# A decoder layer's front: from a planner's order to one written by hand, 76 half tiles of weights with attention staged between them

## The chip, the cores and the metric

The kernel runs on one core of a Trainium2 chip. TensorE does the matrix products, VectorE and ScalarE the elementwise work, GpSimd some elementwise work and some transfers; SyncE issues the transfers of the weights. Each engine takes its instructions from a queue of its own, in order. The metric is the device time of one execution in microseconds (us).

## The reference

One layer of a decoder with 256 tokens, width 2048 and float32 weights. Two kinds of attention read the same normed input, eight latent heads (MLA) and sixteen window heads (SWA) with sinks and a relative bias; then comes an MLP of width 8192.

```python
a = rms_norm(h, attn_norm)
c_q, c_kv, k_rope, q_s, k_s, v_s = split(a @ w_in)
# latent heads: causal softmax over all keys
q  = rms_norm(c_q, q_a_norm) @ w_q_b       # 8 x (128 plain + 64 rotated)
kv = rms_norm(c_kv, kv_a_norm) @ w_kv_b    # 8 x (128 keys + 128 values)
s  = (q_nope . k_nope + rope(q_rope) . rope(k_rope)) * 192 ** -0.5
y_mla = softmax(causal(s)) @ v
# window heads: 16 queries, 2 keys and values, 128 tokens back, a sink per head
s = q_s . k_s * 64 ** -0.5 + rel_bias[t5_bucket(pos_q - pos_k)]
m = max(max(s), sink);  e = exp(s - m)
y_swa = e / (sum(e) + exp(sink - m)) @ v_s
h = h + concat(y_mla, y_swa) @ w_out
h = h + square(relu(rms_norm(h, mlp_norm) @ w_up)) @ w_down
out = rms_norm(h, final_norm)
```

## The kernel before

Every activation and every weight is split into a high and a low part, so that three products of reduced precision make one of full precision. A weight part of 128 x 1024 values is loaded by SyncE into `raw`, copied to its high part `hi` on ScalarE (line 104) and subtracted to its low part `lo` on VectorE (line 105). `raw`, `hi` and `lo` have four buffers each. One chunk of a product is a pair of matmuls, 512 and 256 columns (lines 114 and 116). `load_block` loads two parts, `mm_tile` multiplies a whole tile.

The front goes in this order. `in0` (lines 252 to 271): keys, values and the first two query tiles of the window heads, in 16 chunks as the input arrives. 15 tiles of `w_in` (lines 519 to 558): six query tiles, four tiles of `c_kv`, four of `c_q`, one of the rotated key. Two blocks each of `w_kn` (latent keys) and `w_v` (latent values), three of `w_q_b`; then `w_out` in two halves of 16 tiles, the first over the window heads' output, the second over the latent heads'. The MLP follows: 64 tiles of `w_up` and 64 of `w_down`, two weight parts each.

Attention lies between these tiles. `buckets` makes the bucket of each token distance in 16 compare steps, `lanes_load` spreads them, `bias_step` makes a one-hot row from them and multiplies it with the bias table, and `bias_load` brings the result back through DRAM. `x_norm` makes the norm of the input and scales keys, values and queries by it. For each of eight window head pairs `swa_scores` does the split, the scores and the softmax (lines 380 to 429), and `swa_pv` the transposes and the product with the values (lines 431 to 450). For a latent head `mla_split`, `mla_scores` and `mla_pv` do the same (lines 600 to 663). `c_norm` norms the latent tiles, `rope` rotates. GpSimd subtracts the low parts of queries and keys (lines 387, 604 and 613), rotates (lines 508 and 509) and adds squares (line 187).

The calls are written in the order above, but the order in each engine's queue is the planner's: the framework takes from the written program what it expects to be ready, the earliest written first.

## Time and profile before

| | us |
|---|---|
| three runs | 1030.43, 1031.1, 1032.51 |
| their median | 1031.1 |
| the profiled execution | 1032.6 |
| its span, first to last instruction | 1030.8 |
| TensorE busy in it | 1008.3 |
| VectorE busy | 705.0 |
| ScalarE busy | 539.5 |
| GpSimd busy | 105.7 |

The profile is one execution. Its views used here are the page's busy times, a table of busy time per stretch, the list of waits of an engine, groups of equal instructions, and the timeline. A matmul's end is modelled, and matmuls overlap at their ends, so a duration is longer than the step from one matmul to the next. The first matmul of the `w_in` tiles starts at 30.4 us, the first of `w_out` at 202.1, the first of `w_up` at 308.1.

### The profile page before, as it was taken

To read this page: it belongs to the slowest core of one execution; us is meant where nothing else is said; L and a number is where in the kernel's file an instruction comes from. 1 tells how busy PE (TensorE), PEld (TensorE's weight loads), DVE (VectorE), ACT (ScalarE), POOL (GpSimd) and SP (SyncE) were. 2 spreads that over 40 slices of the span, in tenths; PEclk is the share of its full clock that TensorE was granted. 3 is DMA by queue.
4 is the path that set the end of the run, shared out by engine and by line. 5 is a ranking of instruction groups with operands and counts; after the bars stand their busy time and mean duration, and the time that the engine had idled before them with its cause. 6 is when DMAs were issued, how large, how long until landed. Compare 5 with 4: busy or idle time off the path is not lost.

```text
span 1030.8 us, 15494 instructions
## 1 busy us (share of the span) xinstructions
PE 1008.3 (98%) x5854; PEld 886.8 (86%) x5854; DVE 705.0 (68%) x1123; ACT 539.5 (52%) x893; POOL 105.7 (10%) x112
## 2 busy tenths in 40 slices
PE   9989789999999999999999999999999999999997
PEld 8878678889888888888888888888888888888887
DVE  7895589798897866655566656566666556666664
ACT  6675599965664444333444433344443334445553
POOL 2121340551232200000000000000000000000000
PEclk9999899999999999999999999999999999999999
DMA  8957523353454655555555555555555555555552
GB/s 299 317 206 210 155 91 141 135 188 129 161 185 164 216 192 185 193 193 187 187 195 191 185 192 195 184 189 198 186 185 195 192 185 191 196 185 187 194 172 82
DMA packets 53450, 191.04 MB, mean 185 GB/s; under 512 B 6096, under 2 KB 6480, under 8 KB 52864
## 3 DMA queue, kind: packets, MB, share of 16 engines
q1 hardware_dynamic: 51840, 184.57, 51.1%
q0 software_dynamic: 1392, 5.41, 2.2%
q8 instruction: 46, 0.75, 0.3%
q14 instruction: 28, 0.23, 0.1%
q10 hardware_dynamic: 144, 0.07, 0.0%
HBM read 185.80 MB, written 4.23 MB: 184 GB/s over the span
## 4 chain that ended last, share of the span: by engine, by line
PE 85%; DMA 4%; DVE 4%; ACT 4%; issue 2%; POOL 0%; ACTq 0%; POOLq 0%; DVEq 0%
PE up L114 23%; PE dn L114 22%; PE up L116 12%; PE dn L116 11%; PE wo L114 5%; PE wo L116 3%; DMA raw_in<-in_w_in_dram 2%; DMA bias<-bias_scratch 2%; PE in L114 2%; DVE lo_in L105 1%; PE in L116 1%; PE dn L764 1%; PE yp L444 1%; ACT st L422 0%; DVE buck L243 0%
## 5 line engine op out<-in xcount | busy, mean ns | idle before, releaser
L114 PE MATMUL up<-ms,hi_up 128*128 128x512 f32 x1024 | 355.4, 392 | 0.0
L116 PE MATMUL up<-ms,lo_up 128*128 128x256 f32 x1024 | 287.7, 281 | 0.0
L104 ACT CAST hi_dn<-raw_dn 128x1024 fp32r<-128x1024 f32 x128 | 134.3, 1049 | 201.6 <-PE dn L114 161.2
L105 DVE TENSOR_TENSOR lo_up<-raw_up,hi_up 128x1024 fp32r<-128x1024 f32 x128 | 161.1, 1259 | 114.0 <-ACT hi_up L104 113.6
L114 PEld LDWEIGHTS up<-ms,hi_up 128*128 128x128 f32 x1024 | 192.1, 188 | 42.1
L104 ACT CAST hi_up<-raw_up 128x1024 fp32r<-128x1024 f32 x128 | 134.2, 1049 | 174.3 <-issue 133.6
L105 DVE TENSOR_TENSOR lo_dn<-raw_dn,hi_dn 128x1024 fp32r<-128x1024 f32 x128 | 156.9, 1226 | 96.1 <-ACT hi_dn L104 91.0
L116 PEld LDWEIGHTS up<-ms,lo_up 128*128 128x128 f32 x1024 | 192.5, 188 | 0.0
L114 PE MATMUL dn<-usB,hi_dn 128*128 128x512 f32 x496 | 174.9, 392 | 0.0
L114 PE MATMUL dn<-usC,hi_dn 128*128 128x512 f32 x496 | 174.9, 392 | 0.0
L116 PE MATMUL dn<-usB,lo_dn 128*128 128x256 f32 x496 | 139.4, 281 | 0.0
L116 PE MATMUL dn<-usC,lo_dn 128*128 128x256 f32 x496 | 139.4, 281 | 0.0
L114 PEld LDWEIGHTS dn<-usB,hi_dn 128*128 128x128 f32 x496 | 93.1, 188 | 20.4
L114 PEld LDWEIGHTS dn<-usC,hi_dn 128*128 128x128 f32 x496 | 93.1, 188 | 20.4
L116 PEld LDWEIGHTS dn<-usB,lo_dn 128*128 128x128 f32 x496 | 93.2, 188 | 0.0
L116 PEld LDWEIGHTS dn<-usC,lo_dn 128*128 128x128 f32 x496 | 93.2, 188 | 0.0
L114 PE MATMUL wo<-ys,hi_wo 128*128 128x512 f32 x256 | 90.5, 395 | 0.2 <-DVE mla L323 0.2
L114 PE MATMUL in<-xs,hi_in 128*128 128x512 f32 x240 | 86.9, 400 | 0.0
L116 PE MATMUL wo<-ys,lo_wo 128*128 128x256 f32 x256 | 72.4, 284 | 0.0
L116 PE MATMUL in<-xs,lo_in 128*128 128x256 f32 x240 | 68.8, 287 | 0.7 <-DVE lo_in L105 0.7
L105 DVE TENSOR_TENSOR lo_in<-raw_in,hi_in 128x1024 fp32r<-128x1024 f32 (+1 forms) x39 | 47.7, 1224 | 17.4 <-ACT hi_in L104 17.2
L114 PEld LDWEIGHTS wo<-ys,hi_wo 128*128 128x128 f32 x256 | 48.0, 188 | 10.4 <-DVE mla L323 0.5
(298 smaller groups left out, 1261.3 us busy)
## 6 DMA issues: line engine op xcount, KB each, us to landing
raw_up<-in_w_up_dram SPq DMA_DIRECT2D x128, 512.0 KB, 3.6
raw_dn<-in_w_down_dram SPq DMA_DIRECT2D x128, 512.0 KB, 3.6
raw_in<-in_w_in_dram SPq DMA_DIRECT2D x37, 512.0 KB, 6.0
raw_wo<-in_w_out_dram SPq DMA_DIRECT2D x32, 512.0 KB, 4.2
raw_qb<-in_w_q_b_dram SPq DMA_DIRECT2D x6, 512.0 KB, 3.7
xt<-in_x_tok_dram SPq DMA_DIRECT2D x2, 1024.0 KB, 8.1
bias_scratch<-biasT POOLq DMA_DIRECT2D x4, 512.0 KB, 5.3
bias<-bias_scratch POOLq DMA_DIRECT2D x4, 512.0 KB, 9.9
```

What stands on the lines that cost most here:

```text
L104: nc.scalar.copy(hi[:, :n], raw[:, :n])
L105: nc.vector.tensor_tensor(lo[:, :n], raw[:, :n], hi.bitcast(F32)[:, :n], op=ALU.subtract)
L114: nc.tensor.matmul(ps[:, 0:2 * S], lhsT=hi[:, col:col + P], rhs=act(k, 0, 2 * S), start=first, stop=False)
L116: nc.tensor.matmul(ps[:, S:2 * S], lhsT=lo[:, col:col + P], rhs=act(k, 0, S), start=False, stop=last)
L444: nc.tensor.matmul(yp[:, 0:S], lhsT=v_sc[:, 0, t // 4, j, :], rhs=pt[:, j, 0:2, :].rearrange("p i c -> p (i c)"), start=(j == 0), stop=False)
L764: nc.tensor.matmul(ps[:, b * S:(b + 1) * S].rearrange("p (a c) -> p a c", a=2), lhsT=hi[:, (k % 8) * P:(k % 8 + 1) * P], rhs=x[:, :, b, :] ...
```

## The change

Everything after `in0` and before the MLP is written as one region in which each engine's instructions run in the order in which they are written. The unit is a half: one weight part of 128 x 1024, 76 of them (30 of `w_in`, 4 of `w_kn`, 4 of `w_v`, 6 of `w_q_b`, 32 of `w_out`). A half's matmuls are eight pairs (twelve products of 512 columns for `w_v`). Tables say which step stands ahead of a half's weights (`pre`), which goes into its matmuls at which pair (`hook`), and which follows (`post`).

Besides: the bucket steps are gone, the one-hot row is made from the distance itself by `abs(distance - middle) < half width` of each bucket; the bias goes out and back in pieces of 16 rows; the input's norm loads in four pieces of 1024 columns through the `raw` buffers. The norms are folded: the window scores are scaled per query while the bias is added, values while they are copied from their transposes, and the latent tiles aren't scaled at all, with the `EPS` under their own root scaled instead. The softmax's last scaling goes from ScalarE to one VectorE operation. The product with the values writes two heads into the two partition halves with 64 weight columns each; the first block's and the previous block's share go through one product, with the own block's values replaced by a difference. All subtractions, rotations and adds of GpSimd go to VectorE. The squares for the MLP's norm and the scaling of `h` move into the first 16 `w_up` tiles.

```diff
-    def buckets(step):
...
+    def distances():
...
+        nc.vector.tensor_scalar(dist, n_f[:, 0:2, :], 0.0, 255.0, op0=ALU.max, op1=ALU.min)
+        nc.gpsimd.dma_start(scratch.rearrange("i q c -> q i c"), dist)
...
+    def oh_away(n):
...
+        nc.scalar.activation(oh, lanes[o // 4096][:, o % 4096:o % 4096 + 512], AF.Abs,
+                             bias=c_sb[:, 4:5])
+    def oh_hot(n):
+        nc.vector.tensor_scalar(oh, oh.bitcast(F32), c_sb[:, 5:6], None, op0=ALU.is_lt)
...
+    def swa_max(t):
...
+        for w, other in ((1, bias[:, 0, hs, :]), (0, st[:, :, 0, :])):
+            nc.vector.scalar_tensor_tensor(st[:, :, 0, :], av[:, :, w, :], rx8[:, 0:1], other,
+                                           op0=ALU.mult, op1=ALU.add)
...
+    def swa_norm(t):
...
+        nc.vector.tensor_tensor(st4, st4, l.unsqueeze(2).broadcast_to([P, 4, P]), op=ALU.mult)
...
+    def swa_pv(t):
...
+            nc.tensor.matmul(yp[j * 64:(j + 1) * 64, 0:S], lhsT=vv[:, 0, kv],
+                             rhs=pt[:, j, :, :].rearrange("p i c -> p (i c)"),
+                             start=True, stop=False)
...
+    def mla_lo(hd):
...
+            nc.vector.tensor_tensor(qk[:, i, 0, :], mla[:, row, :], qk.bitcast(F32)[:, i, 1, :],
                                     op=ALU.subtract)
...
+    for i in range(15):
+        e = 2 * i + 2
+        if i < 6:
+            at(pre, e, q_out, 2 + i)
+        elif i < 14:
+            which, c = ("kv", i - 6) if i < 10 else ("q", i - 10)
+            at(pre, e, c_out, which, c, i)
+            at(post, e + 1, c_square, which, c)
...
+            at(pre, e, wo_out, half, mt)
...
+    for n in range(16):
+        s_ = 2 + n // 2
+        at(post, s_, oh_away, n)
+        at(pre, s_ + 1, oh_hot, n)
+        pe(s_ + 1, 3 + 3 * (n % 2), bias_mm, n)
+        at(pre, s_ + 2, bias_out, n)
+    at(post, 13, bias_mask)
...
+    at(post, 16, k_lo)
+    for t in range(8):
+        b = 17 + 3 * t
+        at(pre, b - 1, lambda t=t: stack_hi(f"qs{t}", q_sb[t]))
+        at(post, b - 1, lambda t=t: stack_lo(f"qs{t}", q_sb[t]))
+        pe(b, 1, swa_mm, t)
+        at(post, b, swa_max, t)
+        at(pre, b + 1, swa_exp, t)
+        at(post, b + 1, swa_norm, t)
+        pe(b + 2, 1, swa_turn, t)
+        at(post, b + 2, swa_pt, t)
+        pe(b + 3, 1, swa_pv, t)
+        at(post, b + 3, y_out, NH_MLA + t)
+    for which, s_, g0, sc, dst in (("kv", 22, G_KV, 1.0, ckv_at),
+                                   ("q", 30, G_Q, (128 + 64) ** -0.5, cq_at)):
+        pe(s_, 3, c_sums, which)
+        at(post, s_, c_mean, which)
+        at(pre, s_ + 1, rsqrt_a, which)
+        at(post, s_ + 1, c_scales, which, sc)
+        pe(s_ + 2, 3, bcast, which)
+        for i in range(LC):
+            at(post, s_ + 2 + i // 2, c_apply, which, i, g0)
+            at(pre, s_ + 3 + i // 2, c_hi, which, i, dst)
+            at(post, s_ + 3 + i // 2, c_lo, which, i, dst)
...
+    for hd in range(8):
+        a = 41 + 2 * hd
+        at(post, a, mla_hi, hd)
+        at(pre, a + 1, mla_lo, hd)
+        pe(a + 1, 3, mla_mm, hd)
+        at(post, a + 1, mla_max, hd)
+        at(pre, a + 2, mla_exp, hd)
+        at(post, a + 2, mla_norm, hd)
+        pe(a + 3, 1, mla_turn, hd)
+        at(post, a + 3, mla_pt, hd)
+        pe(a + 4, 1, mla_pv, hd)
+        at(post, a + 4, y_out, hd)
...
+    with tc.manual_schedule():
+        for n in range(3):
+            w_hi(n)
+        for n in range(2):
+            w_lo(n)
+        for s_ in range(NS + 2):
+            for f in pre.get(s_, ()):
+                f()
+            if s_ + 3 < NS:
+                w_hi(s_ + 3)
+            if s_ + 2 < NS:
+                w_lo(s_ + 2)
+            if s_ < NS:
+                mms[s_](s_, weights.pop(s_))
+            for f in post.get(s_, ()):
+                f()
```

`w_hi(n)` issues the load of half `n` and its copy on ScalarE, `w_lo(n)` its subtraction on VectorE. `pe(s, k, f)` puts `f` ahead of pair `k` of half `s`. `stack_hi` and `stack_lo` split a query tile; `mla_hi` and `mla_lo` a latent head's query and key, and for even heads the rotated query as well.

## Rows read from the trace of the kernel before

**Rows 1.** The page's part 1: busy us, share of the span, instructions.

```profile
PE 1008.3 (98%) x5854; PEld 886.8 (86%) x5854; DVE 705.0 (68%) x1123; ACT 539.5 (52%) x893; POOL 105.7 (10%) x112
```

**Rows 2.** Busy time by stretch: us, busy per engine, clock, DMA share, GB/s.

```profile
30.40:100.00 69.60, 66.36 (x375) 56.63 (x374) 53.49 (x101) 46.77 (x75) 15.07 (x21) 1.00 0.75 237
100.00:130.00 30.00, 23.27 (x127) 20.12 (x127) 15.15 (x38) 16.21 (x47) 10.64 (x10) 0.89 0.62 160
130.00:202.00 72.00, 67.70 (x390) 58.25 (x388) 61.39 (x148) 69.07 (x187) 22.93 (x24) 1.00 0.33 117
202.00:308.10 106.10, 105.41 (x633) 93.42 (x634) 95.92 (x178) 67.09 (x133) 36.97 (x34) 1.00 0.48 168
...
400.00:700.00 300.00, 300.00 (x1732) 264.35 (x1732) 184.14 (x240) 126.06 (x152) 0.00 (x0) 1.00 0.54 190
```

**Rows 3.** Waits of TensorE: us in total, times, the longest.

```profile
PE tp L435 <- ACT st L428: 4.4, 1, 4.4
...
PE sb L396 <- DVE st L404: 2.4, 1, 2.4
```

**Rows 4.** Timeline of TensorE, 127 to 136: start, us, instruction.

```profile
127.18 1.02 PE L444 MATMUL yp<-pt,v_sc 128*128 128x256 f32 x4
...
128.49 0.50 PE L195 MATMUL ts_kv<-ones,acc_kv 128*128 128x1 f32 x4
128.85 0.48 PE L392 MATMUL sa<-kk,qs 128*128 128x256 f32 x2
...
129.64 0.28 PE L116 MATMUL in<-xs,lo_in 128*128 128x256 f32 x1
129.76 0.40 PE L114 MATMUL in<-xs,hi_in 128*128 128x512 f32 x1
...
134.73 0.60 PE L435 MATMUL tp<-ident,st 128*128 128x128 f32 x4
135.08 0.48 PE L114 MATMUL in<-xs,hi_in 128*128 128x512 f32 x1
```

**Rows 5.** Timeline of TensorE at 218, a latent head's scores and the transposes after.

```profile
218.00 0.28 PE L625 MATMUL ms<-qk 128*128 128x256 f32 x1
...
218.94 0.49 PE L652 MATMUL mtp<-ident,mst 128*128 128x128 f32 x3
```

**Rows 6.** Timeline of TensorE at 55, bias matmul (64 weight columns) and next pair.

```profile
55.05 0.39 PE L302 MATMUL bias<-oh,rel_hi 128*64 128x512 f32 x1
...
55.51 0.39 PE L114 MATMUL in<-xs,hi_in 128*128 128x512 f32 x1
```

**Rows 7.** Timeline of VectorE at 425, in the MLP; the second needs the first.

```profile
425.78 0.42 DVE L683 TENSOR_TENSOR h<-dn,h 128x256 f32<-128x256 f32 x1 [0.59 <-PE dn L116]
426.24 0.42 DVE L684 TENSOR_TENSOR h<-dn,h 128x256 f32<-128x256 f32 x1
426.75 1.23 DVE L105 TENSOR_TENSOR lo_dn<-raw_dn,hi_dn 128x1024 fp32r<-128x1024 f32 x1
```

**Rows 8.** Timeline of VectorE at 139, steps that don't wait for one another.

```profile
139.41 0.41 DVE L403 TENSOR_TENSOR st<-sa,bias 128x256 f32<-128x256 f32 x1
...
141.06 0.68 DVE L409 TENSOR_REDUCE nm<-st 128x4 f32<-128x512 f32 x1
```

**Rows 9.** Groups of ScalarE, 0 to 330: busy us, mean ns, idle before.

```profile
L104 ACT CAST hi_wo<-raw_wo 128x1024 fp32r<-128x1024 f32 x32 | 33.3, 1048 | 14.6 <-PE wo L114 12.9 <-ACT ms L137 0.6 <-ACT hi_wo L104 0.6
```

**Rows 10.** Timeline of ScalarE at 133, the first exponential and what follows the fourth.

```profile
133.69 0.40 ACT L422 ACTIVATE st<-st,nm 128x128 f32<-128x128 f32 x1
...
135.44 0.80 ACT L142 CAST ckvn<-cn_kv 128x256 fp32r<-128x256 f32 x2
```

**Rows 11.** Groups of GpSimd: busy us, mean ns, idle before.

```profile
L604 POOL TENSOR_TENSOR qk<-mla,qk 128x256 fp32r<-128x256 f32 x16 | 16.9, 1076 | 30.6 <-ACT qk L603 23.4 <-issue 7.1
```

**Rows 12.** The page's part 6, transfers: times, KB each, us to landing.

```profile
bias_scratch<-biasT POOLq DMA_DIRECT2D x4, 512.0 KB, 5.3
bias<-bias_scratch POOLq DMA_DIRECT2D x4, 512.0 KB, 9.9
```

More of the change, by code (lines that the diff above doesn't have):

```diff
@@ new lines, in diag, with bcast @@
+    def diag(name):
+        for b in range(2):
+            dg = work.tile([P, P], F32, tag="diag", name=f"dg_{name}_{b}", bufs=2)
+            nc.vector.tensor_scalar(dg, ident, box[f"y_{name}"][:, b:b + 1], None, op0=ALU.mult)
+            box[f"dg_{name}_{b}"] = dg
+    def bcast(name):
+        ps = misc_ps(f"bc_{name}")
+        for b in range(2):
+            nc.tensor.matmul(ps[:, b * P:(b + 1) * P], lhsT=ones, rhs=box[f"dg_{name}_{b}"],
+                             start=True, stop=True)
+        box[f"bc_{name}"] = ps
@@ new lines, in wo_mm, with mm, in0_out, q_out @@
+    def wo_mm(half, mt):
+        def mm(s_, w):
+            ps = dense_ps(f"wo{half}_{mt}")
+            act = view(ys[1 - half])
+            for k in range(8):
+                run_hooks(s_, k)
+                pair(ps, w, k * P, act, k, k == 0, k == 7)
+            opened[f"wo{half}_{mt}"] = ps
+        return mm
+    def in0_out(j):
+        t = evac_sum(ps0[j], f"in0_{j}")
+        nc.vector.tensor_tensor(first[j], ps0[j][:, 0:S], t, op=ALU.add)
+    def q_out(t):
+        q_sb[t] = work.tile([P, S], F32, tag="q_s", name=f"q_s{t}", bufs=8)
+        sum_evac(q_sb[t], opened.pop(t - 2), f"q{t}")
@@ new lines, in v_out, with wo_out, ms_hi @@
+    def v_out(b):
+        for tb in range(2):
+            nc.scalar.copy(box["mla"][:, VV + 4 * tb + 2 * b:VV + 4 * tb + 2 * b + 2, :],
+                           opened[f"v{b}"][tb].rearrange("p (a c) -> p a c", a=2))
+    ms_box = []
+    def wo_out(half, mt):
+        residual(opened.pop(f"wo{half}_{mt}"), mt)
+    def ms_hi(mt):
+        if not ms_box:
+            ms_box.append(big.tile([P, KC, 2 * S], F32R, tag="A", name="ms"))
+        nc.scalar.activation(ms_box[0][:, mt, 0:S], h[:, mt, :], AF.Copy,
+                             scale=g_sb[:, G_MLP + mt:G_MLP + mt + 1])
@@ new lines @@
+    W0 = len(srcs)
+    for half in range(2):
+        for mt in range(KC):
+            e = plan(w_out[half, mt // 2][:, (mt % 2) * WH:(mt % 2 + 1) * WH], wo_mm(half, mt)) + 1
+            at(pre, e, wo_out, half, mt)
+            if half == 1:
+                at(post, e, ms_hi, mt)
+                at(pre, e + 1, ms_lo, mt)
+    NS = len(srcs)
+    for j, s_ in ((2, 0), (3, 0), (0, 1), (1, 1)):
+        at(pre, s_, in0_out, j)
+    at(pre, 2, rope_a)
+    at(pre, 3, rope_b, 0)
+    at(pre, 4, rope_b, 1)
@@ new lines @@
+    at(pre, 5, rope_c)
+    at(post, 5, rope_d)
+    for n in range(16):
[5 more added lines that the diff above has]
+    at(post, 13, bias_mask)
+    for n in range(4):
+        at(pre, 9 + n, x_piece, n % 2, n // 2)
+    at(pre, 13, x_mean)
+    at(pre, 13, rsqrt_a, "x")
+    at(pre, 14, x_scales)
+    pe(14, 2, v_turn)
+    pe(14, 6, bcast, "x")
+    at(pre, 15, x_apply)
@@ new lines @@
+    at(pre, 15, v_scale)
+    at(post, 15, k_hi)
+    at(post, 15, v_diff)
+    at(post, 16, k_lo)
[11 more added lines that the diff above has]
+        at(post, b + 3, y_out, NH_MLA + t)
```

633 lines of the change are left out of this document (351 added, 282 removed).

## The prediction

> **What bounds the kernel now.** I read the page's busy shares first. TensorE is busy 98% of the span [rows 1], so no change can give more than TensorE's idle and slow time, unless it takes matmuls away. The windows by stage, cut where the work changes (input groups to 30.4 us, `w_in` tiles to about 149, `w_kn`, `w_v` and `w_q_b` to 202, `w_out` to 308.1, then the MLP), show where that time lies [rows 2]: 3.2, 6.7, 4.3 and 0.7 us idle in the four windows between 30.4 and 308.1, 15.0 in all, and from 400 us on none. In 100:130 the granted clock is 0.89 on the mean, so for some of it the lower level, 1.2 GHz, after a wait of 4.4 us; 11% of 30 us is another 3.3 us. The waits of TensorE name the causes [rows 3]: transposes waiting for a softmax, scores waiting for VectorE.
>
> How much could go? I price the matmuls alone. A pair (512 and 256 columns) takes 300 us / 866 pairs = 0.3464 us where nothing is idle [rows 2]. A head pair of the window attention takes 1.31 us for `swa_pv`'s products (127.18 to 128.49), 0.79 for the scores (128.85 to 129.64), 0.35 for four transposes (134.73 to 135.08) [rows 4]: 2.45. A latent head takes 0.94 for its scores (218.00 to 218.94) [rows 5], three quarters of 0.35 for its transposes and half of 1.31 for its products: 1.85. A 512-column matmul alone takes half of 0.46 [rows 6]. From 30.4 us: 576 pairs 199.5, 48 of `w_v` 10.9, 32 for the bias 7.3, 8 head pairs 19.6, 8 heads 14.8, some 2.3 for the norms; together 254.4. They would end at 284.8 and they end at 308.1: **23.3 us** is lost, of which the windows show 18.3 and the rest is the drain before each wait. That is all the change can win, as it takes no matmul away.
>
> **What the change does to each engine.** TensorE keeps all its matmuls. The spots at which it asks for attention operands are now fixed: one pair into a half, or three. The MLP and the tail stay, except that 15 adds and the scaling of `h` go from GpSimd to VectorE in the first 16 `up` tiles; VectorE is busy 184 of 300 us in such a stretch [rows 2], so I cost them at nothing; without that cover they are some 11 us of VectorE.
>
> VectorE loses the 16 bucket steps, the scaling by the input norm of 6 tiles and 11 projections, and the masking of the previous block. It gains 56 two-input operations that GpSimd does now (40 low parts of queries and keys, 10 steps of rotations, 6 folds of squares), and the softmax's last scaling, from ScalarE. GpSimd's take 1.08 us each [rows 11], VectorE's 0.42 and a weight subtraction 1.23 [rows 7].
>
> **How the queues go.** In written order each half is the same: evacuations and conversions (`pre`), the weight copy for three halves on (ScalarE) and subtraction for two halves on (VectorE), the half's matmuls, then `post`. `pre` waits for the last matmul of the half before. So an engine starts each half when TensorE does, and what stands last in `post` must be done when TensorE reaches the next half's first hook. My rules: a 256-wide VectorE operation lasts 0.42 and the next, if independent, issues 0.33 later (139.41 to 141.06 for five) [rows 8]; a dependent one comes 0.46 later [rows 7], a hand-over of 0.04, which I round to 0.05; a reduction lasts 0.68 [rows 8]; ScalarE copies a half in 1.05 [rows 9]; four exponentials take 1.75 (133.69 to 135.44) [rows 10]; a matmul's result comes 0.16 after its issue slot (0.28 - 0.12) [rows 4]. A half of eight pairs is 2.77 us.
>
> **Halves 2 to 10** (bias). The one-hot compare stands behind the rotation's angle steps (four 256-wide operations, three dependent ones, three and a clamp). In half 3 they take 1.4 us ahead of it and half 2 has run over, so the bias matmul waits 1.5; in half 4 with an evacuation ahead as well, 2.2; then 0.5 in three halves that have an evacuation. Sum **5.1**. The key norm and first stacks, halves 14 to 17: four key subtractions and two stack ones, 2 us, follow the weight in half 16: **1.6**.
>
> **Window attention** (halves 17 to 41, three to a head pair). From the end of its scores: result at 0.21; mask and bias steps 0.48 + 0.35 + 0.48 + 0.48, reduction 0.73, two small ones 0.42, so 3.15; sink 0.1 and four exponentials to 4.98; sum, reciprocal, the 512-wide scaling (0.69) to 6.24. TensorE meanwhile issues 7 + 8 + 1 = 16 pairs, 5.54 us, then asks for the scaled scores: at least 0.70 lost, eight times, **5.6**. Twice (halves 21 and 27) the square of a latent tile stands on ScalarE behind exponentials and weight copy, and its add on VectorE ahead of the scaling: 1.5 each, **3.0**. And VectorE is too full. Its issue time for a head pair is three weights at 1.14, 3.4, and 5.4 for the steps above, the stack, the masked own block and the output's low part, against TensorE's 3 x 2.77 + 2.45 = 10.8. Where the latent norms, the rotated key and the `w_kn` evacuations fall, 4.3 (halves 23 to 25), 4.5 (29 to 31) and 5.2 (32 to 34) come on top: 13.1, 13.3 and 14.0, over by 2.3, 2.5 and 3.2, **8.0**, most of it not recoverable as every group has a hook that needs the newest result. That is 16.6; walking the three queues operation by operation by the same rules gives 17.5, the longest wait 4.1 in half 28. I take **17.5**.
>
> **Latent attention** (halves 41 to 59). In every second half TensorE asks for split operands after a pair, 0.26 of transposes and two pairs: 1.30. VectorE first adds the residual twice (0.21 to 1.09), then subtracts: two for an odd head, ready at 1.81, four for an even one, at 2.47. Waits of 0.5 and 1.2: 5.8 for seven heads. The first head finds VectorE behind with the query rotation: 2.6, and 1.7 at its transposes. Sum **10.1**. The other 16 `w_out` halves: VectorE needs 1.14 + 0.80 + 0.41 = 2.35 of 2.77; no wait.
>
> **The sum.** 5.1 + 1.6 + 17.5 + 10.1 = 34.3 us lost where 23.3 are lost now: the front ends 11.0 later by the sums, 11.3 by the walk (319.4 against 308.1). I take 11.3. The profiled execution took 1032.6 us (span 1030.8), 1.5 above the median of 1031.1; on the median this gives **1042.4**.
>
> **Prices the trace doesn't show.** The bounds of the walk: with all VectorE durations 10% shorter it loses 4.8 less, 10% longer 9.1 more. The bias now goes back in 16 small reads as it is made. Before, writes landed in 5.3 us and big reads in 9.9 [rows 12]. From the last copy, in half 11, 5.3 and at most 9.9 make 15.2 us, beside issue and masking; the first scores ask for it six halves, 16.6 us, later: 0 to 4.4, the wait it makes now [rows 3]; I take 0, to which 15.2 is nearer. `xt` comes in four pieces beside the weights: 2.1 MB at 237 GB/s [rows 2] are 8.8 us, less two halves of lead: 0 to 3.3. The lanes are loaded in the first 30 us, 1 MB: 0 to 4.4. I take 0 for both, as before's DMAs were busy 0.75 at most of the stretch after [rows 2]. A wait of 4.1 like the one that halved the clock: 0 to twice 3.3; I take 0, as the other queues catch up meanwhile. Products with 64 weight columns, the two heads into the two partition halves: the nearest row, the bias matmul with 64 columns, shows no gap before the next pair and none saved [rows 6]; I take 0. The Trainium skill's "TensorEngine Tiling (Array Packing)", Tiling Modes, has a rule for them: different tiles run in parallel, and changing the mode drains the engine. If the two heads ran in parallel, the products would halve and, in the walk, 1.4 us go; two drains of 0.16 a group would add 1.7. The row shows neither, having only one tile.
>
> **The rivals.** (a) *Slack enough, not slower*: the four weight buffers let VectorE run ahead, hooks find their operands ready, and the written order ends what now costs 23.3 us. For it: the two longest waits of now, 4.4 and 2.4 [rows 3], hang on the late bias, which goes. Against: evacuations tie VectorE to TensorE each second half at least, and each hook asks for the newest result. With half my waits (17) the front ends 6 us earlier: 1025; with the eight unavoidable ones and few others (8) 1016. It decides if the losses stay under 23.3, two thirds of mine; in the walk even VectorE durations 20% shorter don't bring that. Chance 0.20. The Trainium skill's "GPSIMD Engine Reference", Engine selection, speaks for this rival: two-input elementwise work belongs on VectorE, GpSimd being about twice as slow. The trace agrees on the operation, 1.08 against 0.42; by it alone 56 operations save 37 us of engine time; but TensorE hardly waited for GpSimd. (b) *Slower still*: DMA arrives late (bias, pieces) or the clock halves once or twice, 4 to 14 more: 1047 to 1057. Chance 0.18. (c) *No change*: waits as long as now, 1029 to 1033: 0.08, among it 0.03 for an order that in effect stays what it was. (d) My forecast, 1033.2 to 1047: 0.54.
>
> **How the numbers follow.** About 0.2%, 2 us, is what can be told from no change. Faster (a) 0.20; same (c) 0.08; slower (b) and (d) 0.72. The likeliest case's own range is 1034 to 1050; as cases of both signs count, the range goes to 1018, leaving out half of (a), and to 1056.
>
> **What would show it.** Right: in the waits of TensorE, transposes of both attentions waiting for VectorE's scaling, eight times each 0.7 us or more in the first, scores of the second waiting 0.5 and 1.2 in turn; the first `up` matmul near 319 us; VectorE's busy share higher between 100 and 200 us, GpSimd near nothing. Wrong: waits of the window transposes absent (the chain is shorter than 5.5 us), or `up` starting before 308. A wait for `bias` of over 2 us, or a clock below 1.00 in a stretch of the front, would be (b).

## The result, and the profile after

The changed kernel takes **1065.3 us** (median of four, 1064.6 to 1071.1) against 1031.8 for the kernel before on the same chip: a ratio of **1.0334, with a 95% interval of 1.0292 to 1.0376**. It is 33.5 us slower where 11.3 were forecast: the sign was right, the forecast size a third of the measured one, and the time lies outside the range, whose upper end was 1056.

The profiled execution has a span of 1063.1 us. The page's part 1, as in [rows 1]:

```profile
PE 1016.1 (96%) x5854; PEld 885.2 (83%) x5854; DVE 715.7 (67%) x1165; ACT 541.9 (51%) x883; POOL 23.2 (2%) x47
```

Busy time by stretch of the changed kernel, the columns and nearly the cuts of [rows 2]; the last two are the end of the front and a piece of the MLP:

```profile
30.40:100.00 69.60, 58.06 (x303) 48.31 (x302) 39.63 (x72) 48.29 (x83) 13.54 (x21) 0.93 0.78 227
100.00:130.00 30.00, 24.88 (x155) 20.76 (x154) 24.38 (x50) 20.60 (x47) 0.00 (x0) 1.00 0.40 141
130.00:202.00 72.00, 57.61 (x313) 46.37 (x312) 58.27 (x134) 46.33 (x118) 0.00 (x0) 0.93 0.30 107
202.00:308.10 106.10, 98.78 (x570) 84.41 (x570) 90.28 (x197) 64.50 (x148) 0.00 (x0) 0.97 0.36 127
308.10:339.90 31.80, 31.80 (x185) 28.00 (x184) 30.41 (x55) 19.99 (x33) 0.00 (x0) 1.00 0.57 198
400.00:700.00 300.00, 300.00 (x1733) 264.42 (x1732) 187.66 (x243) 126.65 (x153) 0.00 (x0) 1.00 0.55 189
```

The MLP is as it was. All the loss lies ahead of the first `up` matmul, which starts at 339.9 (308.1 before, 319.4 forecast). TensorE is idle 11.5 + 5.1 + 14.4 + 7.3 = 38.4 us there, against 15.0, and three of the four stretches have a clock under 1.00, against one. The waits of TensorE from 30 to 345 us, as in [rows 3]:

```profile
PE tp L490 <- DVE st L484: 15.4, 6, 5.6
PE bc_x L366 <- DVE dg_x L360: 6.1, 1, 6.1
PE ms L642 <- DVE qk L629: 4.5, 7, 2.9
PE bias L297 <- DVE oh L292: 2.3, 1, 2.3
PE yp L507 <- ACT pt L496: 2.2, 1, 2.2
PE bias L297 <- ACT oh L286: 2.0, 1, 2.0
```

The transposes of the window heads (`tp`) wait for the scaled softmax, the latent scores (`ms`) for the low parts, the first bias matmuls for the one-hot row: these were forecast, though the last line, also for the one-hot row, is ended by ScalarE's step and not by VectorE's. The second line, the broadcast of the input norm, and the fifth, the window products, were not. The cause of the broadcast's wait stands on ScalarE (timeline of ScalarE in the changed kernel: start, length, instruction; in brackets the idle time before it and what ended it):

```profile
77.88 1.05 ACT L958 CAST hi<-raw 128x1024 fp32r<-128x1024 f32 x1 [3.45 <-DMA raw<-in_w_in_dram]
...
83.45 1.06 ACT L340 ACTIVATE xt<-xt 128x1024 f32<-128x1024 f32 x1 [1.31 <-DMA xt<-in_x_tok_dram]
84.42 0.19 ACT L340 ACTIVATION_READ_ACCUMULATOR xt<-xt 128x1 f32 x1
87.61 1.04 ACT L958 CAST hi<-raw 128x1024 fp32r<-128x1024 f32 x1 [3.00 <-DMA raw<-in_w_in_dram]
88.67 1.28 ACT L344 ACT_TABLE_LOAD   x1
89.96 0.20 ACT L344 ACTIVATE sq_x<-ms_x 128x2 f32<-128x2 f32 x1
```

Weights and pieces of `x` land late, ScalarE waits for each in order, and the root that the broadcast needs stands behind them. Nothing but its place makes it wait for a weight.

### The profile page after: what moved, and what is told of

Its sections match the earlier page's. It is cut to its first block, busy times and chain, and to the rows that moved or that the text cites. A ratio compares the mean times of both kernels' runs of the same rounds, so it can differ in the third digit from the quotient of the medians.

```text
span 1063.1 us, 15321 instructions
## 1 busy us (share of the span) xinstructions
PE 1016.1 (96%) x5854; PEld 885.2 (83%) x5854; DVE 715.7 (67%) x1165; ACT 541.9 (51%) x883; POOL 23.2 (2%) x47
## 4 chain that ended last, share of the span: by engine, by line
PE 83%; DVE 6%; ACT 6%; DMA 3%; issue 1%; SPq 0%; ACTq 0%; DVEq 0%
PE up L114 22%; PE dn L114 21%; PE up L116 11%; PE dn L116 11%; PE wo L735 5%; PE wo L737 3%; PE in L735 2%; ACT hi L958 2%; DMA raw<-in_w_in_dram 1%; PE in L737 1%; ACT st L474 1%; DMA raw_in<-in_w_in_dram 1%; DVE lo L964 1%; PE dn L1046 1%; PE ms L647 1%
## 5 line engine op out<-in xcount | busy, mean ns | idle before, releaser
L105 DVE TENSOR_TENSOR lo_up<-raw_up,hi_up 128x1024 fp32r<-128x1024 f32 x128 | 156.8, 1225 | 118.5 <-ACT hi_up L104 117.9
L958 ACT CAST hi<-raw 128x1024 fp32r<-128x1024 f32 x76 | 79.4, 1045 | 39.9 <-PE wo L735 12.1
L964 DVE TENSOR_TENSOR lo<-raw,hi 128x1024 fp32r<-128x1024 f32 x76 | 94.4, 1242 | 8.0 <-PE in L737 4.3
L116 PEld LDWEIGHTS dn<-usB,lo_dn 128*128 128x128 f32 x496 | 93.2, 188 | 0.0
L116 PEld LDWEIGHTS dn<-usC,lo_dn 128*128 128x128 f32 x496 | 93.2, 188 | 0.0
L735 PE MATMUL wo<-ys,hi 128*128 128x512 f32 x256 | 92.5, 401 | 0.0
L735 PE MATMUL in<-xs,hi 128*128 128x512 f32 x240 | 89.5, 410 | 0.0
L737 PE MATMUL wo<-ys,lo 128*128 128x256 f32 x256 | 72.4, 283 | 0.0
L737 PE MATMUL in<-xs,lo 128*128 128x256 f32 x240 | 69.0, 287 | 0.0
```

The source lines that it names most:

```text
L105: nc.vector.tensor_tensor(lo[:, :n], raw[:, :n], hi.bitcast(F32)[:, :n], op=ALU.subtract)
L116: nc.tensor.matmul(ps[:, S:2 * S], lhsT=lo[:, col:col + P], rhs=act(k, 0, S), start=False, stop=last)
L735: nc.tensor.matmul(ps[:, 0:2 * S], lhsT=hi[:, col:col + P], rhs=act(k, 0, 2 * S), start=first, stop=False)
L737: nc.tensor.matmul(ps[:, S:2 * S], lhsT=lo[:, col:col + P], rhs=act(k, 0, S), start=False, stop=last)
L958: nc.scalar.copy(hi, raw)
L964: nc.vector.tensor_tensor(lo, raw, hi.bitcast(F32), op=ALU.subtract)
```

## Where the time went, stage by stage

The starts of the first products of each kind, read from the timelines of TensorE, cut the front into five stages (us). "Walk" is the prediction's walk of the three queues by its rules: its figures are calculated, no run shows them. "Moved" is the order of the fifth experiment below.

| | first window scores | to the 8th | to the first latent scores | to the 8th | to `up` | `up` starts |
|---|---|---|---|---|---|---|
| walk of the prediction | 92.6 | 93.2 | 18.0 | 58.7 | 56.9 | 319.4 |
| changed kernel | 102.8 | 99.9 | 18.2 | 61.9 | 57.1 | 339.9 |
| walk, moved | 85.9 | 81.8 | 16.4 | 55.0 | 56.9 | 295.9 |
| e5, moved | 99.1 | 83.7 | 16.4 | 57.1 | 57.1 | 313.4 |
| e10, moved, no bias trip | 94.7 | 81.7 | 16.4 | 57.2 | 57.1 | 307.0 |
| e13, e10 without lanes | 92.3 | 81.7 | 16.4 | 57.1 | 57.1 | 304.6 |

(In e5 one of the first scores' products ran 2.4 us ahead and the rest waited for the keys; the later start is given.) Of the 20.5 us that the walk missed, 10.2 lie ahead of the first scores, 6.7 in the window stage, 3.2 in the latent one.

## The experiments

Theory A: the loss comes from the positions in which the steps are written, and what the waits there bring with them. Theory B: the redesign (half tiles, work moved to VectorE) costs it. Within A, the suspects for what the walk had missed: late pieces of `x`, the half clock, one wait on VectorE, the bias's way through memory. The times, and the ratios to the kernel before measured beside them (the changed kernel's own ratio, 1.0334, is known to 0.0042, some 4 us):

| run | us | ratio, 95% |
|---|---|---|
| e1, planner's order | 1040.0 | 1.0091 (1.0070 to 1.0111) |
| e2, pieces of `x` early | 1062.2 | 1.0309 (1.0279 to 1.0339) |
| e3, clock kept up | 1062.7 | 1.0311 (1.0290 to 1.0332) |
| e4, own block first | 1063.3 | 1.0310 (1.0288 to 1.0332) |
| e5, four moves | 1036.4 | 1.0053 (1.0033 to 1.0072) |
| e6, e5 and pieces early | 1037.6 | 1.0065 (1.0042 to 1.0088) |
| e7, planner, pieces early | 1031.8 | 1.0017 (0.9997 to 1.0038) |
| e8, e2 without the bias trip | 1061.2 | 1.0305 (1.0282 to 1.0327) |
| e9, e6 and writes ahead | 1036.9 | 1.0052 (1.0034 to 1.0069) |
| e10, e6 without the bias trip | 1032.0 | 1.0012 (1.0000 to 1.0023) |
| e11, first move alone | 1056.7 | 1.0251 (1.0235 to 1.0267) |
| e12, second move alone | 1059.1 | 1.0266 (1.0246 to 1.0286) |
| e13, e10 without lanes | 1028.9 | 0.9984 (0.9973 to 0.9996) |
| e14, e9 and rotation later | 1031.8 | 1.0017 (1.0000 to 1.0033) |
| e15, planner, keys' latent first | 1031.4 | 1.0003 (0.9984 to 1.0021) |
| e16, e15 and rotation later | 1030.5 | 0.9989 (0.9976 to 1.0001) |

**Order against redesign (e1).**

```diff
-    with tc.manual_schedule():
+    if True:
```

> The changed kernel with the written order taken away: the same operations, half tiles, folded norms and pieces, but the planner sets the order of each queue, as in the kernel before. Theory A (the loss comes from the positions of the written order, and from what the waits there bring with them): the longest waits go, the front ends between 302 and 315 us, time 1022 to 1040 us. Theory B (the loss is in the redesign, work moved to VectorE and half tiles): the time stays within 8 us of the changed kernel's 1065, 1057 or more.

It came to 1040.0, the upper end of A's range: by the ratios 25 of the 33.5 us are the order. The waits that are left, TensorE's two longest in e1, and ScalarE's longest between 60 and 100 us:

```profile
PE bias L297 <- ACT biasT L303: 10.9, 3, 6.8
PE bc_kv L366 <- DVE dg_kv L360: 3.3, 1, 3.3
```
```profile
ACT xt L340 <- DMA xt<-in_x_tok_dram: 6.9, 2, 6.5
```

The planner too puts the squares of `x` ahead of the bias copies and then waits for a late piece. So where the pieces are written costs time under the planner as well; e7 below moves them.

**The suspects one at a time (e2, e3, e4, e8).**

```diff
-        at(pre, 9 + n, x_piece, n % 2, n // 2)
+        at(pre, 2 + 2 * n, x_piece, n % 2, n // 2)
```

> The four pieces of x for the input norm load in halves 2, 4, 6 and 8 instead of 9, 10, 11 and 12; nothing else moves. Theory A (they crowd the weights and the bias transfers between 60 and 96 us, ScalarE is blocked on late weights, the root of the norm stands behind it, and TensorE waits 6.1 us for the norm's broadcast, after which it runs 6.9 us at half clock): wait and half clock go, some 6 + 3 = 9 us, time about 1056. Rival (the bias's own transfers crowd, and the pieces are only beside them): under 3 us, 1062 or more; a mere shift of the lateness to halves 2 to 8 would also show so.

The wait for the broadcast is gone, 60 to 100 us has 37.2 us of TensorE and a clock of 1.00 (33.1 and 0.91 in the changed kernel), and the first scores come 8.6 us earlier, at 94.2. But the time fell by 3, not 9. In the window stage that follows, 108.0 us are needed instead of 99.9. The wait of VectorE that is new there, between 85 and 128 us, and the stage in the changed kernel and in e2:

```profile
DVE st L451 <- POOL bias L315: 2.9, 1, 2.9
```
```profile
102.80:202.74 99.94, 81.54 (x462) 66.30 (x463) 80.70 (x177) 65.39 (x163) 0.00 (x0) 0.95 0.32 112
94.22:202.23 108.01, 87.34 (x462) 70.80 (x462) 81.02 (x177) 65.41 (x163) 2.00 (x1) 0.89 0.35 110
```

The bias, whose mask (its last step, on GpSimd) was done in time while the scores were late, is now late itself. And of the 8.1 us more, 5.8 are the same matmuls at a lower clock (0.89 instead of 0.95), 2.3 are more idle time of TensorE. Whether the gain would stay with the clock kept up isn't tested: early pieces and filled waits weren't run together.

e8 takes the bias's way through memory away as well (the transfers are left out, zeros stand in the bias):

```diff
-        if e == 3:
+        if e == 4:
...
+    nc.gpsimd.memset(bias, 0.0)
```

> The written order, the pieces of x in halves 2, 4, 6 and 8, and the bias's way out to memory and back left out, 4 writes and 16 reads, with zeros in the bias: its time is that of the order without the late transfers. Theory A (the gain of the early pieces was eaten by the bias, for which VectorE waited 2.9 us until its mask was done at 99 us): the first head pair's waits fall, and what is left is the queues' own, some 323 to 327 for the end of the front, time 1049 to 1053. Rival (the queues give it back between 100 and 200 us whatever the transfers do): 1059 or more.

The rival held: one us less, which the intervals can't tell from none. `up` starts at 335.4, with 14.3 us of waits of the transposes left (15.4 in the changed kernel). In this order what the transfers no longer cost is waited for elsewhere.

e3 puts products of a constant ahead of the hooks that wait:

```diff
+    def fill(ps, n):
+        for i in range(n):
+            nc.tensor.matmul(ps[:, 0:P], lhsT=ones, rhs=ones, start=True, stop=True)
...
+        fill(tp, {3: 24, 5: 28}.get(t, 0))
```

> No wait is taken away: TensorE multiplies a constant by itself, with the result overwritten, ahead of the five hooks whose waits precede the half clock (8 or 9 such products of about 0.16 us ahead of two bias matmuls, 30 ahead of the input norm's broadcast, 24 and 28 ahead of the transposes of head pairs 3 and 5, 12 ahead of the first latent scores), each time less than the wait lasts. Theory A (the half clock has a price of its own): of the six stretches at half clock, 27.3 us, those filled make 23.9; at most half of that, 12 us, comes back, I expect 6 to 12, time 1053 to 1059. Rival (TensorE at half clock only lets the other queues catch up, the same time is then waited at later hooks): 0 to 3 us, 1062 or more, with the granted clock near 1.00 in the front.

In the changed kernel two of its six stretches at the lower level, 1.2 GHz, read so (windows: us, TensorE busy first, then the others, the clock after GpSimd):

```profile
89.00:95.80 6.80, 2.87 (x10) 2.58 (x11) 5.13 (x13) 4.43 (x8) 2.87 (x5) 0.52 1.00 245
150.40:157.20 6.80, 4.86 (x17) 4.31 (x18) 5.32 (x10) 2.93 (x7) 0.00 (x0) 0.52 0.42 157
```

All six make 27.2 us, with TensorE busy for 20.3 of them; at a clock of about 0.53 that is 20.3 x 0.47 = 9.5 us of TensorE's time. In e3 the clock is higher, but three stretches of 3.4 us at the lower level are left or new (from 103.1, 171.1 and 229.8 us):

```profile
60.00:100.00 40.00, 37.63 (x234) 32.80 (x232) 19.77 (x34) 26.38 (x46) 10.60 (x15) 1.00 0.99 266
100.00:130.00 30.00, 24.01 (x140) 20.14 (x141) 22.98 (x47) 19.30 (x45) 0.00 (x0) 0.94 0.36 118
130.00:149.00 19.00, 18.08 (x114) 15.35 (x114) 17.10 (x42) 11.06 (x31) 0.00 (x0) 1.00 0.33 110
149.00:202.00 53.00, 49.93 (x320) 42.60 (x319) 42.69 (x94) 36.77 (x92) 0.00 (x0) 0.97 0.33 110
```

The time is 2.6 us lower, under the 6 to 12 of the theory, inside the rival's 0 to 3, and within the interval. After the filled wait ahead of the broadcast the first scores come at 102.0 instead of 102.8, so up to there the time at the lower level, 10.2 us in the changed kernel, cost hardly anything. The window stage takes 99.7 us instead of 99.9, with 6.8 us at the lower level instead of 10.2.

e4 swaps two operations:

```diff
+        nc.vector.tensor_tensor(own, tp..., mask_ownT..., op=ALU.mult)
         nc.scalar.copy(pt.rearrange("p j i c -> p (j i c)"), tp)
-        nc.vector.tensor_tensor(own, tp..., mask_ownT..., op=ALU.mult)
```

> The masked own block, which VectorE reads from the transposed scores, is written ahead of ScalarE's copy of them. In the changed kernel VectorE's step waits for the copy each time, though it needs nothing of it. Theory A (this wait holds VectorE up, above all where ScalarE has the root and the rotation's copies, and its backlog makes TensorE wait 5.6 us for the transposes of head pair 5): the walk of the queues gives 3.6 less, and the half clock after that wait, 3.4 us, may go with 1.7: time 1060 to 1062. Rival (ScalarE then waits for VectorE instead): within 1.5 us of 1065.

The changed kernel has VectorE's step behind ScalarE's copy of the same tile, and that copy behind the root's table and the rotation's copies (first VectorE's line, then ScalarE's queue before it):

```profile
171.60 0.42 DVE L498 TENSOR_TENSOR own<-tp,mask_ownT 128x256 f32<-128x256 f32 x1 [3.81 <-ACT pt L496]
```
```profile
166.86 1.28 ACT L344 ACT_TABLE_LOAD   x1
168.15 0.20 ACT L344 ACTIVATE sq_q<-ms_q 128x2 f32<-128x2 f32 x1
168.37 1.65 ACT L595 COPY rt_kr<-kr 32x256 f32<-32x256 f32 x4
170.04 1.04 ACT L958 CAST hi<-raw 128x1024 fp32r<-128x1024 f32 x1
170.99 0.58 ACT L496 COPY pt<-tp 128x512 f32<-128x512 f32 x1
```

Both only read `tp`, yet they run one after the other, in the order in which they are written: VectorE waited 6.8 us in four head pairs; in e4 the roles are exchanged and ScalarE waits 4.4 us for VectorE. From the 6th to the 7th scores, where ScalarE had that backlog, the swap gave 4.1 us (18.4 to 14.3). But the other head pairs took as much longer: the window stage is 99.8 us against 99.9, with TensorE idle 2.9 us less and its matmuls 2.8 us longer, at a clock of 0.91 instead of 0.95. The time fell by 2.

What became shorter in e4 is the latent stage, and by its clock. The stage from the first to the 8th latent scores has the same instructions in the changed kernel, in e3 and in e4 (in this order):

```profile
220.90:282.78 61.88, 58.16 (x325) 49.55 (x326) 54.43 (x126) 35.88 (x85) 0.00 (x0) 0.94 0.33 119
219.78:280.20 60.42, 56.54 (x326) 48.33 (x326) 54.24 (x126) 35.90 (x85) 0.00 (x0) 0.97 0.38 122
222.82:281.72 58.90, 55.03 (x325) 46.92 (x325) 54.24 (x126) 35.67 (x85) 0.00 (x0) 1.00 0.38 125
```

With two stretches of 3.4 us at the lower level it takes 61.9 us, with one 60.4, with none 58.9, where the walk, which has no half clock, gives 58.7. Here each stretch costs about 1.5 us; in the moved order below the stage takes 57.1 with one (e5) and 55.6 with none (e6).

Each suspect alone is worth 1 to 3 us, no more than the intervals can tell, though each wait did go or shrink: the next hook asks for a result that is late too (e8), or the half clock comes elsewhere (e2, e4).

**Four positions (e5).**

```diff
-            at(pre, e, q_out, 2 + i)            # c_out likewise
+            at(pre, e + 1, q_out, 2 + i)
-            if s_ + 3 < NS: w_hi(s_ + 3)        # after pre
+            if s_ + 3 < NS: w_hi(s_ + 3)        # after post
-        pe(b + 2, 1, swa_turn, t)               # pt, pv, y_out likewise
+        pe(b + 3, 1, swa_turn, t)
-        at(pre, a + 1, mla_lo, hd)
+        at(post, a, mla_lo, hd)
-        at(pre, b - 1, ... stack_hi); at(post, b - 1, ... stack_lo)
+        at(post, b - 3, ... stack_hi); at(pre, b - 2, ... stack_lo)
```

> Still the written order and all operations of the changed kernel; four positions move. ScalarE's weight copy goes behind the half's matmuls and the evacuations of the query and latent tiles go one half later; the window transposes, products and outputs go one half later; the latent low parts go ahead of the half's end; the query stacks go two halves earlier. Theory A (the positions make the waits, and the queues have room): the prediction's walk, with the wait of the masked block for ScalarE's copy put in, ends the front 27.5 us earlier by these four, time 1038, at most 1044 as the transfers between 60 and 96 us stay late. Rival (a wait that goes comes back at the next hook, as it did where the pieces came early, where 6.1 became 3, or where the clock was held): 1055 or more. Theory B (the redesign's work is too much for VectorE): 1055 or more too, with VectorE busy over 0.95 between 150 and 200 us.

It came to 1036.4: 29 us faster than the changed kernel by the two ratios, where the walk had 27.5, with no operation taken away. Waits of TensorE, and windows, of e5:

```profile
PE bc_x L366 <- DVE dg_x L360: 2.9, 1, 2.9
...
PE tp L490 <- DVE st L484: 1.8, 2, 0.9
...
PE ms L642 <- DVE qk L629: 0.5, 1, 0.5
```
```profile
149.00:202.00 53.00, 47.26 (x271) 37.41 (x270) 48.72 (x111) 43.18 (x112) 0.00 (x0) 1.00 0.37 123
202.00:300.00 98.00, 95.42 (x567) 84.70 (x566) 89.34 (x194) 59.65 (x126) 0.00 (x0) 0.98 0.46 151
```

The transposes wait 1.8 us instead of 15.4, the latent scores 0.5 instead of 4.5. Between 149 and 202 us VectorE is busy 0.92, 48.7 of 53, against 41.1 in the changed kernel, where TensorE waited for it: it had room for the work and was kept from it. Theory B falls for this loss: both of its signs are absent.

**One move alone (e11, e12)**: the first two entries of that diff, and the third.

> Of the four moves the first alone: ScalarE's weight copy behind the half's matmuls and post steps, and the evacuations of the query and latent tiles one half later. Theory A (the evacuation, which waits for the last matmul of the half before, holds up all that stands behind it): the walk gives 10.8, time 1053 to 1056. Rival (the chain of the window softmax is too long for its 16 pairs, so the evacuations' place matters little): 1061 or more.

> Of the four moves the second alone: window transposes, products and outputs one half later, so that the softmax chain has 24 pairs and not 16 between scores and transposes. If the chain of 6.24 us against 5.54 makes the loss, as the prediction had it: 5.6 and more, with the waits of the transposes (15.4 us) gone to under 4, time 1057 or less. If the queues' backlog makes it: the waits move to the scores, which ask for VectorE's stacks, and to the products, and the walk gives 5.5 at most: 1059 to 1065.

By the ratios (1.0334 less 1.0251, of 1031) the first gives 8.6 us (the walk had 10.8), the second 7.0, the four 29. The other two were not run alone, so what they give, and what only the four together give, isn't told apart. e12 shows the transfer of a wait, in TensorE's list:

```profile
PE sb L436 <- DVE qs L426: 7.5, 5, 3.0
...
PE tp L490 <- DVE st L484: 2.3, 2, 1.6
```

The chain got its 24 pairs and its waits fell from 15.4 to 2.3; the scores, 1.1 in the changed kernel, now wait 7.5 for the stacks, which stand in the same queue. So the chain's length and the queues' backlog both count: the gain is over the 5.5 of the one account, the time, 1059.1, over the 1057 of the other.

**The transfers once the order has room (e6, e9, e10, e13).** e6 is e5 with e2's line; e9 puts each write of the bias ahead of the reads of the rows before; e10 leaves the trip out as e8 does; e13 also the lanes' loads.

```diff
-            for g in range(4):                      # reads of rows b
+            for r in ([b - 1] if b else []) + ([3] if b == 3 else []):
+                for g in range(4):                  # reads of rows r
```
```diff
-            nc.gpsimd.dma_start(lanes[i][g * 32:(g + 1) * 32, :], ...)
+        nc.gpsimd.memset(lanes[i], 0)
```

> The four moved positions, and the pieces of x in halves 2, 4, 6 and 8. Theory A: the wait for the input norm's broadcast goes as well, but the bias, whose mask ended at 99 us when the pieces came early, then bounds the first scores: some 3 to 5 us under the kernel with the four moves alone, 1033 to 1036. Rival (each gain in the first 100 us is given back until 200 us): within 2 us of it.

> The four moved positions, the early pieces of x, and on GpSimd's queue each write of the bias ahead of the four reads of the rows before it. With the pieces early the last write was issued at 81.1 us behind reads that wait for their own write, and VectorE waited 6.6 us for the mask, done at 100.4. Theory A (the bias now ends last where the queues have room): the last write goes some 5 us earlier, the mask ends near 95, the front ends 3 to 6 us earlier, time 1030 to 1034, faster than or equal to the kernel before. Rival (the transfers are limited by what all of them move, not by their order): the mask ends after 99, time within 2 us of the kernel with the pieces early.

> The four moved positions, the early pieces of x, and the bias's way out to memory and back left out, zeros in its place: its time is that of the moved order without that wait. Where the written order stood as in the changed kernel, leaving it out gave 1 us. Theory A (what a late transfer costs depends on whether the queues behind it have room): here it gives 8 to 13 us against the same kernel with the trip, as the walk has 297.7 for the end of the front without the bias and 305.8 with it at 98 us: 1024 to 1030. Rival (additive: the trip costs the same 1 to 2 us in either order): 1034 or more.

> The four moved positions and the early pieces of x; the bias's way out to memory and back is left out, and so are the eight loads that spread the distances over the lanes (1 MB in the first 45 us); constants stand in their place. Without the way but with the lanes, the first window scores come at 94.7 us, where the walk has them at 85.9; ScalarE waits there three times for weights that land late, 6.1 us. Theory A (what the walk misses ahead of the first scores is late transfers): the scores come at 86 to 90, the front ends at 298 to 302, time 1022 to 1027. Rival (it is the bias steps' own order, the rotation's angle steps ahead of the compare): within 2 us of the kernel with the lanes.

e6 gave nothing over e5 by the medians (in the two profiled executions `up` starts 3.4 us earlier): the first scores come at 91.7 and VectorE then waits 6.6 us for the mask. GpSimd's queue, last write, last reads and mask, in e6 and then in e9:

```profile
81.06 0.56 POOL L306 DMA_DIRECT2D bias_scratch<-biasT  x1
91.64 2.26 POOL L311 DMA_DIRECT2D bias<-bias_scratch  x4 [10.01 <-DMA bias_scratch<-biasT]
98.42 2.01 POOL L315 TENSOR_SCALAR_AFFINE_SELECT bias<-bias 128x2048 f32<-128x2048 f32 x1 [4.51 <-issue]
```
```profile
76.68 0.57 POOL L306 DMA_DIRECT2D bias_scratch<-biasT  x1 [5.62 <-ACT biasT L303]
...
86.44 2.23 POOL L312 DMA_DIRECT2D bias<-bias_scratch  x4 [6.41 <-DMA bias_scratch<-biasT]
97.96 2.04 POOL L316 TENSOR_SCALAR_AFFINE_SELECT bias<-bias 128x2048 f32<-128x2048 f32 x1 [9.29 <-DMA bias<-bias_scratch]
```

The last reads are issued 5.2 us sooner and the mask starts only 0.5 sooner, with a DMA share of 0.96 in e6 and 0.99 in e9 between 60 and 100 us: the rival's signs held. That the sum of the transfers is the limit isn't shown by this, for in e14 below, with the transfers of e9 and a share of 0.93, the last reads go out 4.4 us sooner than in e9 (at 82.0) and the mask starts 6.1 sooner. Without the trip (e10) 5.6 us come off e6, against 1.0 in the old order: not the 8 to 13 that I expected, but not additive either. The lanes are another 3.1 (e13), and there neither expectation held: the first scores come at 92.3, where the walk has 85.9, so the bias's way and the lanes are not all that it missed. In the moved order these transfers cost some 9 us; in the old one the trip, the only one taken out there, cost hardly anything.

**The order ahead of the first scores (e14), and the best order for the redesign (e7, e15, e16).**

```diff
-    at(pre, 2, rope_a)     # rope_b 3 and 4, rope_c and rope_d 5
+    at(pre, 10, rope_a)    # 11 and 12, 13
```
```diff
-    for i in range(15):
+    for pos, i in enumerate((0, 1, 2, 3, 6, 7, 8, 9, 4, 5, 10, 11, 12, 13, 14)):
```

> As the kernel with the writes of the bias ahead, and the rotation's angle steps, which stand ahead of the one-hot compare in halves 2 to 5, in halves 10 to 13. Theory A (late transfers make the losses ahead of the first scores): within 2 us of that kernel. Rival (the angle steps hold up the compare, as the prediction had it, 3.7 of the 5.1 us of the bias halves): the waits of the first bias matmuls go, the bias is on its way 2 to 4 us earlier and the front ends as much earlier, 1032 to 1034.

> The planner's order of the changed operations, with the pieces of x written in halves 2, 4, 6 and 8. With the planner and the pieces late, 10.9 us of waits for the bias copies on ScalarE and a half clock of 0.91 stood between 60 and 100 us. Theory A (the pieces hold ScalarE up there): these go, 1030 to 1034, no slower than the kernel before. Rival (the bias's own 16 writes and reads crowd the transfers): 1037 or more.

> The planner's order of the changed operations, pieces of x early, bias writes ahead, and the four latent tiles of the keys and values ahead of the last two query tiles, with their norm four halves earlier. Under the planner's order TensorE's longest wait was for that norm, 3.5 us, in a stretch of 19 us with 7.3 idle and a clock of 0.79. Theory A (with the planner only operands that come late cost time): wait and half clock go, 6 to 10 us, 1022 to 1027, faster than the kernel before. Rival (the planner runs out of other work there, whatever the norm does): within 3 us of 1032.

> As the planner's order with the latent tiles of the keys and values first, and the rotation's angle steps written in halves 10 to 13, behind the one-hot compares, which gave 5 us where the order is written. Theory A (the early losses are the bias steps' own order, and the written place sets it under the planner too, as it takes what was written first): the first bias waits, 2.6 us, go, the bias comes sooner, 1026 to 1029, faster than the kernel before. Rival (the planner already puts the compares first where that is better): within 1.5 us of 1031.

e14 gave 5.1 us over e9 by the medians, 3.6 by the ratios, so the rival's order counts, though by another way than it said: waits of 4.4 us for the bias matmuls stay, but the mask starts at 91.9 instead of 98.0. e7 gave 8 us over e1, as A had it: ScalarE no longer waits for pieces ahead of the bias copies. In e15 the wait for the keys' norm is gone, and `up` starts at 306.9, 4.5 us earlier than in e7 in the profiled executions, but the medians don't differ (1031.4 and 1031.8): its rival held, as e16's did. **No order of the redesign that was tried is measurably faster than the kernel before**; e16's interval, 0.9976 to 1.0001, still holds no change. Why it stops there isn't settled, and no part of the redesign was tried by itself in the kernel before.

## Why the prediction was right in sign and wrong in size

**The step that failed** is the paragraph on prices that the trace of before doesn't show: late transfers and the half clock were each put at 0. In their place the runs showed the first scores 10.2 us later than walked, of which 8.6 came back when the pieces of `x` moved (e2), and a latent stage 3.2 us longer, which is its half clock (e3, e4). A second step failed beside it: the walk has no wait of the masked block for ScalarE's copy, 3.8 us at its longest. The other 2.6 us of the window stage, which has 10.2 us at the lower level, are open.

**The loss before and the place of the new one: right.** All of it is between 30 us and the first `up` matmul; the MLP hides its added VectorE work; most of the waits are those named, ended by the engines named. The 5.0 us that the prediction calls the drain before each wait are not that alone: TensorE's list for the kernel before has 14 waits there, which at 0.16 make 2.2.

**Halves 2 to 10**, 5.1: the bias matmuls wait 2.3 + 2.0 + 1.1 = 5.4. Right as waits (1.5 + 2.2 and three times 0.5 are 5.2, as the terms stand). **Halves 14 to 17**, 1.6: the scores wait 1.1, but the broadcast's 6.1 is not in the sum.

**Window attention**, 17.5: transposes 15.4 + 0.6, products 2.2, the keys' broadcast 0.7, together 18.9. The sum is near; the parts are not. Of the forecast eight waits of the transposes of 0.7 us or more there are five, and two of them make 10.4 of the 16.0:

```profile
152.34 1.09 PE L490 MATMUL tp<-ident,st 128*128 128x128 f32 x4 [4.75 <-DVE st L484]
...
185.49 1.09 PE L490 MATMUL tp<-ident,st 128*128 128x128 f32 x4 [5.64 <-DVE st L484]
```

The first is in half 28, where the walk had its longest, 4.1. The second has the cause that was missed, the wait of the masked block for ScalarE's copy. Put into the walk, it makes the front some 4.1 longer, 323.4, with the longest wait where it was found, ahead of the 6th transposes; e4 took 4.1 away there, but the stage gave it back. **What I called "unavoidable" and "most of it not recoverable" was neither.** They hold only for the written places; e5 got the waits to 1.8 with the same instructions.

**Latent attention**, 10.1: 4.5 + 1.3 + 0.5 = 6.3 of waits (four of 0.5 and three of 1.2 are 5.6, not 5.8, as the terms stand). The first head waits 2.9, where 2.6 were forecast, its transposes 0.5 instead of 1.7. From the third head on the scores come 8.36 and 8.02 us apart in turn, where e5 has 7.52: 0.84 and 0.50 lost, where 1.2 and 0.5 were forecast. The stage is 3.2 longer than walked, and that is the price of its two stretches of half clock.

**The prices taken at 0.** The bias trip, 0 to 4.4: 0 held in the changed kernel (mask started at 94.9, scores at 102.8) only because the scores were late. The pieces, 0 to 3.3, and lanes, 0 to 4.4: here the prediction failed by most. I set them against DMAs "busy 0.75 at most of the stretch after"; but that row is the kernel before's, whose transfers lie elsewhere, and in 60 to 100 us the share is now 0.93. The pieces' place ahead of the root on ScalarE turned it into 6.1 us and most of the 10.2 by which the first scores came late; the lanes were taken out only in the moved order (3.1). The half clock, 0 to twice 3.3: 9.5 us of TensorE's time by the windows. When e3 took away 17 of its 27 us, 2.6 came back; 3.0 is its price in the latent stage alone, by the clock of e4. So it was not 0; that the other queues catch up meanwhile fits what lies ahead of the first scores, where e3 gained 0.8.

**The sum.** Late first scores 10.2, the masked block 4.1, the rest of the window stage 2.6, the latent stage 3.2, the other two 0.4: 20.5 of the front's 339.9 against 319.4. These are differences from the walk, not savings: taken away one at a time, the causes gave 1 to 3 us each, so how the 22 us between forecast and measured time divide among them stays open.

**The rivals.** (b), DMA lateness and clock, named where 13.4 of the 20.5 lie, with a bound of 14 us; its sign, a clock under 1.00 in the front, came. (a), slack enough, was turned down because shorter VectorE durations didn't bring it in the walk. That varied the wrong thing: the same walk, with positions moved, gave 295.9, below the 308.1 of before, and from the first scores on its stages were right to about 2 us (e5). A bound from durations can't tell what a loss made by order can give back.

**The products of 64 columns**, -1.4 to +1.7, taken at 0. Timeline of TensorE in the changed kernel at 128 us:

```profile
127.73 0.28 PE L737 MATMUL in<-xs,lo 128*128 128x256 f32 x1
127.94 0.65 PE L507 MATMUL yp<-pt,vv 128*64 128x256 f32 x4
128.42 0.39 PE L511 MATMUL yp<-own,vv 128*64 128x128 f32 x4
128.74 0.73 PE L436 MATMUL sb<-kk,qs 128*128 128x256 f32 x4
```

They take 128.74 - 127.94 = 0.80 us where the full-width ones took 1.31 [rows 4]: 0.5 less for each head pair, 4 in all of TensorE's time; what the front had of it no run shows. The step from a pair's second matmul to them is 0.21 instead of the 0.12 to the next pair, 0.09 for the change of mode, less than the 0.16 that the prediction priced. The Trainium skill's "TensorEngine Tiling (Array Packing)", Tiling Modes, says that different tiles can run in parallel and that changing the mode drains the engine. The trace agrees with the first, if not to a half: the products of the two heads start within 0.01 us of each other. Of the second it shows no more than the 0.09.

## What to carry to other kernels

In an order written by hand, an operation waits for all that stands ahead of it on its engine; so evacuations, which wait for the last matmul, belong behind the work that other engines ask for next, and a chain needs as many halves as its queues, not its durations, make it long. Taking away one wait showed little here, as the next operand was late too or the clock fell elsewhere, so test moves together, and vary positions, not only durations, before a loss is called unavoidable. Price a transfer by what will run beside it in the changed kernel, and a half clock by whether TensorE sets the pace of that stage.

## What was not expected of the hardware and the language

The 64-column products for two partition halves overlapped: 0.80 against 1.31 us. Two reads of one PSUM tile by ScalarE and VectorE ran one after the other in the written order, for up to 3.8 us of waiting. The Trainium skill's "PSUM — Partial Sum Buffer", section "PSUM bank collisions raise a hardware error", says that reads of one bank by two engines collide too and that the compiler puts a dependency between them. The trace agrees with the dependency, in both written orders (in e4 ScalarE waits); whether the reads would collide no run shows. The prediction had missed this wait. The bias writes of 512 KB landed, on the median, in 6.8 us in the changed kernel and 7.6 in e6, against 5.3 before [rows 12]; the share of the DMAs between 60 and 100 us was 0.93, 0.96 and 0.76. It isn't the share alone: in e9, at 0.99, they took 6.8. And TensorE at 1.2 GHz for 3.4 us cost about 1.5 us in the latent stage, where it sets the pace, and next to nothing ahead of the first scores: 0.8 for 10.2 us.
